# A decoder layer on one core: adaLN modulation from transposed weights, and eight accumulators in the first projection pass

## The chip, the cores and the metric

The kernel runs on one core of one Trainium2 chip. The metric is the device time of one execution in microseconds (us): 1293.14 us before, the median of three runs (1292.88 to 1295.22). One further execution was profiled. All views below are of that one.

The engines of the core run side by side and wait for one another by semaphores: TensorE (PE; PEld is its weight load), VectorE (DVE), ScalarE (ACT), GpSimd (POOL), and SyncE (SP), whose queue issues the DMA transfers.

## The reference, cut to what matters

```python
c_act = silu(c)                              # c: (1, 1024)
mod = c_act @ w_ada + b_ada                  # w_ada: (1024, 6144)
sh1, sc1, g1, sh2, sc2, g2 = split(mod, 6)   # 1024 numbers each
h = x * (1 + sc1) + sh1                      # x: (1024 tokens, 1024)
proj = h @ w_in                              # columns q, kc, vc, ksl, vsl, kwn, vwn, gt, u, v
# kc, vc -> compressed keys and values; v -> gelu, norm, spatial gating with u
# attention (compressed, selected, window), gating, output projection, layer norm
h = x * (1 + sc2) + sh2
out = layer_norm(ALPHA * x + (1 + g2) * ((silu(h @ w1) * (h @ w3)) @ w2))
```

Everything is float32. The kernel multiplies with a high and a low part of each operand: one product tile takes three matmuls, high by high, high by low, low by high (`mm3`, lines 91 to 98).

## The kernel before, in words

The beginning of the kernel makes `h` and multiplies it with the columns `v`, `kc` and `vc` of `w_in`. The model dimension (1024) is cut into eight blocks `k` of 128. For each block, the kernel needs 128 values of `sc1` and of `sh1`, one per partition (`mod`), and the block of `x` with the model dimension on the partitions.

**Modulation.** `load_ada` (153) loads, for each block `k`, the 1024 rows of `w_ada` by 128 columns of `sh1` and of `sc1`, in pieces of 512 bytes. The sum over the 1024 rows is made in two steps. POOL sums the first three groups of 128 rows (325 to 329), DVE the last five (222, 223), DVE adds the two (336). TensorE then transposes the 128 x 256 sum (232) and DVE adds along the row (235) and adds the bias (239). One block at a time is done so (the pair 4 and 5 together, `GR`).

**x.** `load_x` loads `x` with tokens on the partitions. TensorE transposes it, four 128 x 128 pieces to a PSUM tile (`make_t`, 256). ACT makes the high part of `h` from it (243), ACT or DVE the float32 value (245, 247), DVE or POOL the low part (`affine_split`, 241).

**The two passes.** PSUM holds eight banks. In the first pass (lines 322 to 345) there are accumulators for four token tiles of `v` and for `kc` and `vc` over the first 512 tokens, six banks; the others serve the transposes. A block of the first pass is 18 matmuls with 512 columns. The second pass (391 to 401) does the same for the other 512 tokens. ACT and DVE empty the accumulators behind each pass: the copies `kT` (403) and the gelu `vn` (358).

**Behind the passes** come the key compression (`cmp_blk`, `cmp_mm`; line 496 builds its input from `kT` on DVE and POOL), the products with `u` (`pu`), the transposes of `w_s` (`pws`, from `ws`, which POOL masks in line 557), then V, the gates, K and Q (`pq`, with DVE's part in line 686). In between, `bgstep` puts one background step at a time: `ada_row` for `g1`, and `ada_tiles` with `ada_cols` for `sh2` and `sc2`. These last two are 16 row sums on DVE (lines 222 and 223, 128 x 1024 each), then 16 transposes on TensorE (232) into the PSUM tag that `pq` uses too, and DVE's row sums (235).

**What sets the order.** Program order is the priority; a scheduler orders each engine's instructions, and `order` pins one behind another (the loads of the beginning are pinned in a chain, `dseq`). SBUF tiles come from pools: `B` has 41 buffers, `RAW` four; the PSUM tag `g` has three banks, `ot` one, `s` four.

Of the kernel before, what the change touches and what calls it, by code (L numbers as in the profile page):

```python
# [16 lines left out]
S = 1024  # L17
# [14 lines left out]
GR = ((0, 1), (1, 1), (2, 1), (3, 1), (4, 2), (6, 1), (7, 1))  # L32
# [3 lines left out]
UA, PK = 6, 3  # L36
# [7 lines left out]
def hymba_kernel(ctx, tc, x, c, w_ada, b_ada, w_in, cmp_pos, cmp_w1, cmp_w2, vn_g, vn_b, w_s, b_s,  # L44
                 out_g, w_o, ln1_g, ln1_b, w1, w3, w2, ln2_g, ln2_b, out):
# [93 lines left out]
    rows = B("rows")  # L139
    dseq(rows[0:8, 0:128], c.rearrange("o (k p) -> (o k) p", p=128))  # L140
    dseq(rows[0:48, 128:256], b_ada.rearrange("o (k p) -> (o k) p", p=128))
    pc = G("pc")
    nc.tensor.transpose(out=pc[:, 0:8], in_=rows[0:8, 0:128], identity=ident[0:8, 0:8])
    ccol = cst.tile([128, 8], F32, name="ccol")
    V_.tensor_copy(ccol, pc[:, 0:8])
# [3 lines left out]
    V_.tensor_scalar(cact, cact, 0.5, None, MULT)  # L149

    adat, xt = {}, []

    def load_ada(q, n):
        for k4 in range(0, NK, 4 // n):
            t = B("ada")
            tv = t.rearrange("p (k a n) -> p k a n", k=4 // n, a=2)
            for a in range(2):
                dseq(tv[:, :, a, :], w_ada[k4 * 128:(k4 + 4 // n) * 128, a * 1024 + q * 128:a * 1024 + (q + n) * 128]
                     .rearrange("(k p) n -> p k n", p=128))
            for k in range(4 // n):  # L160
                adat[q, k4 + k] = t[:, k * 256 * n:(k + 1) * 256 * n]

    def load_x(hf, j):
        xb = B("x")
        dseq(xb.rearrange("p (t n) -> p t n", t=4),
             x[hf * 512:(hf + 1) * 512, j * 256:(j + 1) * 256].rearrange("(t p) n -> p t n", p=128))
        xt.append(xb)
# [7 lines left out]
    wvr, wkr, wv, wkc, lastw = [], [], [], [], []  # L175

    def load_wv(k2):
        wvr.append(B("wvr"))
        dseq(wvr[k2].rearrange("p (k n) -> p k n", k=2),
             w_in[k2 * 256:(k2 + 1) * 256, OFF["v"]:OFF["v"] + 512].rearrange("(k p) n -> p k n", p=128))  # L180

    def load_wkc(k2):
        wkr.append(RAW("wkr")[:, 0:512])
# [3 lines left out]
    def split_start(q):  # L187
        if q % 2 == 0:
            h, l = split(wvr[q // 2])
            for i in range(2):  # L190
                wv.append((h[:, i * 512:(i + 1) * 512], l[:, i * 512:(i + 1) * 512]))
            h, l = split(wkr[q // 2], 512)
            lastw.append(lasts[0])
            for i in range(2):
                wkc.append((h[:, i * 256:(i + 1) * 256], l[:, i * 256:(i + 1) * 256]))
# [16 lines left out]
    cols = cst.tile([128, 80], F32, name="cols")
    pc = G("pc")
    nc.tensor.transpose(out=pc[:, 0:48], in_=rows[0:48, 128:256], identity=ident[0:48, 0:48])
    V_.tensor_copy(cols[:, 0:48], pc[:, 0:48])
    posT = cst.tile([128, 64], F32, name="posT")
    bcol, l1g, l1b, og, bs = cols[:, 0:48], cols[:, 48:56], cols[:, 56:64], cols[:, 64:72], cols[:, 72:80]
    mod = cst.tile([128, 4, 8], F32, name="mod")
# [6 lines left out]
    def ada_cols(acc, m, j0, c0, n):  # L225

        r = sml.tile([128, 2, n], F32, name="adr")
        p = [G("pm") for _ in range(n // 2)] or [G("pm")]
        for a in range(2):
            for i in range(n):  # L230
                z = a * n + i
                nc.tensor.transpose(out=p[z // 4][:, z % 4 * 128:(z % 4 + 1) * 128], in_=acc[:, a, i * 128:(i + 1) * 128], identity=ident)
        for z, pp in enumerate(p):
            w = min(2 * n, 4)
            V_.tensor_reduce(out=r.rearrange("p a i -> p (a i)")[:, z * 4:z * 4 + w],
                             in_=pp[:, 0:w * 128].rearrange("p (i q) -> p i q", q=128), op=ADD, axis=AX)
        for a in range(2):
            j = j0 + a
            V_.scalar_tensor_tensor(mod[:, m + a, c0:c0 + n], r[:, a, :], float(a), bcol[:, j * 8 + c0:j * 8 + c0 + n], ADD, ADD)
# [12 lines left out]

# [15 lines left out]
    def start_mm(k, hf):  # L268
        for t in range(4):
            sl = slice(hf * 512 + t * 128, hf * 512 + (t + 1) * 128)  # L270
            mm3(acc4[t // 2][:, t % 2, :], (hH[k][:, sl], hL[k][:, sl]), wv[k], k == 0, k == NK - 1)
# [1128 lines left out]
```

## Time and profile before

| | |
|---|---|
| median of three runs | 1293.14 us |
| the profiled execution | 1295.98 us |
| its span, first to last instruction | 1293.9 us |
| PE busy | 1217.3 us, 94% of the span |
| DVE busy | 978.1 us, 76% |
| mean granted TensorE clock | 0.986 |
| DMA | 188.09 MB, mean 145 GB/s |

The span is what the views are drawn on; the execution's time is 2.1 us longer. A matmul's shown duration overlaps the next one's, so that a matmul's share of TensorE's time is read from start to start.

### The profile page before, as it was taken

To read this page: it belongs to the slowest core of one execution; us is meant where nothing else is said; L and a number is where in the kernel's file an instruction comes from. 1 tells how busy PE (TensorE), PEld (TensorE's weight loads), DVE (VectorE), ACT (ScalarE), POOL (GpSimd) and SP (SyncE) were. 2 spreads that over 40 slices of the span, in tenths; PEclk is the share of its full clock that TensorE was granted. 3 is DMA by queue.
4 is the path that set the end of the run, shared out by engine and by line. 5 is a ranking of instruction groups with operands and counts; after the bars stand their busy time and mean duration, and the time that the engine had idled before them with its cause. 6 is when DMAs were issued, how large, how long until landed. Compare 5 with 4: busy or idle time off the path is not lost. (4 is left out here: it accounts for less than half of the span.)

```text
span 1293.9 us, 17271 instructions
## 1 busy us (share of the span) xinstructions
PE 1217.3 (94%) x5980; PEld 1007.1 (78%) x5980; DVE 978.1 (76%) x1702; ACT 569.3 (44%) x1040; POOL 396.2 (31%) x400
## 2 busy tenths in 40 slices
PE   5899999899999999999789999999999989999994
PEld 3687797778888888878567788888788868888873
DVE  5746887959999999868767867667767668785487
ACT  2343422349888998113623323333323225454131
POOL 5332213325655674301132233232233230000123
PEclk8999999999999999999999999999999999999997
DMA  9821453901000002554335645556554579687252
GB/s 288 266 66 50 140 157 101 242 3 66 1 2 1 1 2 73 201 177 128 114 123 170 188 169 165 179 188 187 169 194 142 178 229 342 238 274 258 58 202 81
DMA packets 148011, 188.09 MB, mean 145 GB/s; under 512 B 17402, under 2 KB 95314, under 8 KB 147924
## 3 DMA queue, kind: packets, MB, share of 16 engines
q1 hardware_dynamic: 147924, 187.00, 45.4%
q8 instruction: 47, 0.77, 0.2%
q14 instruction: 40, 0.33, 0.1%
HBM read 136.11 MB, written 48.76 MB: 143 GB/s over the span
## 5 line engine op out<-in xcount | busy, mean ns | idle before, releaser
L777 POOL TENSOR_SCALAR P<-P,ast,gate 128x640 f32<-128x640 f32 (+7 forms) x128 | 99.6, 785 | 66.5 <-DVE ast L776 50.0
L107 DVE TENSOR_TENSOR wL<-cr,wH 128x1024 fp32r<-128x1024 f32 x77 | 99.7, 1318 | 24.8 <-ACT wH L102 24.5
L1058 POOL TENSOR_TENSOR w2r<-w2r,g2r 128x512 f32<-128x512 f32 x44 | 60.9, 1399 | 169.2 <-DMA w2r<-in_w 84.6
L102 ACT ACTIVATE wH<-cr 128x1024 fp32r<-128x1024 f32 x77 | 79.9, 1059 | 70.9 <-DMA cr<-combP 63.1
L107 DVE TENSOR_TENSOR pt<-pt,pt 128x512 fp32r<-128x512 f32 (+1 forms) x148 | 99.9, 682 | 7.0 <-ACT pt L102 6.3
L710 ACT ACTIVATE P<-P,ast 128x640 f32<-128x640 f32 (+7 forms) x128 | 93.8, 734 | 1.7 <-DVE ast L709 1.2
L102 ACT ACTIVATE pt<-pt 128x512 fp32r<-128x512 f32 (+1 forms) x148 | 87.1, 592 | 16.3 <-PE pt L128 13.7
L1169 POOL TENSOR_TENSOR pt<-pt,pt 128x512 f32<-128x512 f32 x22 | 35.0, 1592 | 164.4 <-ACT pt L1168 164.4
L128 PE MATMUL pt<-ident,P 128*128 128x128 f32 x528 | 78.9, 272 | 0.2 <-DVE pt L107 0.2
L1124 DVE TENSOR_TENSOR h<-h,pt 128x512 f32<-128x512 f32 x33 | 26.4, 799 | 66.1 <-POOL pt L1171 65.7
L128 PEld LDWEIGHTS pt<-ident,P 128*128 128x128 f32 x528 | 65.1, 140 | 12.7 <-issue 0.5
L1112 PE MATMUL pcd<-wH,wH 128*128 128x512 f32 x176 | 69.2, 395 | 4.7 <-ACT pt L1163 2.4
L102 ACT ACTIVATE wH<-raw 128x1024 fp32r<-128x1024 f32 (+2 forms) x41 | 42.3, 1040 | 69.8 <-DMA combP<-wt 20.4
L1276 PE MATMUL py<-wH 128*128 128x512 f32 x176 | 68.6, 394 | 2.6 <-DVE r L1215 2.6
L1112 PE MATMUL pa<-h2H,wH 128*128 128x512 f32 x176 | 68.9, 392 | 0.8 <-ACT pt L1147 0.3
L1114 PE MATMUL pa<-h2H,wL 128*128 128x512 f32 x176 | 68.9, 391 | 0.7 <-DVE wL L107 0.7
L1113 PE MATMUL pcd<-wL,wH 128*128 128x512 f32 x176 | 69.2, 393 | 0.0
L1114 PE MATMUL pcd<-wH,wL 128*128 128x512 f32 x176 | 69.0, 392 | 0.0
L1276 PE MATMUL py<-wH,wL 128*128 128x512 f32 x176 | 69.0, 393 | 0.0
L1276 PE MATMUL py<-wL,wH 128*128 128x512 f32 x176 | 68.9, 392 | 0.0
L1113 PE MATMUL pa<-h2L,wH 128*128 128x512 f32 x176 | 68.5, 389 | 0.0
L107 DVE TENSOR_TENSOR wL<-raw,wH 128x1024 fp32r<-128x1024 f32 (+2 forms) x41 | 51.6, 1265 | 19.8 <-ACT wH L102 15.9
(323 smaller groups left out, 3671.3 us busy)
## 6 DMA issues: line engine op xcount, KB each, us to landing
cr<-combP SPq DMA_DIRECT2D x77, 512.0 KB, 4.9
ada<-in_w_ada SPq DMA_DIRECT2D x96, 256.0 KB, 4.2
raw<-in_w SPq DMA_DIRECT2D x48, 512.0 KB, 4.9
w2r<-in_w SPq DMA_DIRECT2D x44, 256.0 KB, 2.8
combP<-wt SPq DMA_DIRECT2D x44, 256.0 KB, 3.5
combP<-as SPq DMA_DIRECT2D x44, 256.0 KB, 2.4
combP<-w2r SPq DMA_DIRECT2D x33, 256.0 KB, 2.0
combP<-h SPq DMA_DIRECT2D x33, 256.0 KB, 3.9
```

The costliest lines, as they stand in the source:

```text
L102: A_.activation(o, i, AF.Copy)
L107: return V_.tensor_tensor(o, i, f(h), SUB)
L128: nc.tensor.transpose(out=p[:, j * 128:(j + 1) * 128], in_=src(j), identity=ident)
L710: A_.activation(P, P, AF.Exp, scale=-1.0, bias=nm, accum_out=den)
L777: P_.tensor_scalar(P, P, st[:, 2, hh:hh + 1], gcol(i, h, br), MULT, MULT)
L1058: P_.tensor_tensor(r[z][a], r[z][a], rowt["g2r"][:, a * 512:a * 512 + 512], MULT)
L1112: nc.tensor.matmul(o, lh, rh, start=start and i == 0, stop=False, skip_group_check=not start)
L1113: nc.tensor.matmul(o, lh, rl, start=False, stop=False, skip_group_check=not start)
L1114: r = nc.tensor.matmul(o, ll, rh, start=False, stop=i == 3, skip_group_check=not start)
L1124: V_.tensor_tensor(s, s, c, MULT)
L1169: P_.tensor_tensor(p5, p5, p7, ADD)
L1276: lastm[0] = nc.tensor.matmul(o, x_[:, ts_], y_[:, 512:1024], start=not cont and p == 0 and n == 0, stop=p == NP - 1 and n == 2, skip_grou ...
```

## The change: what it does

The host lays out three more inputs: `xT`, the transpose of `x`; `w_adaT`, the transpose of `w_ada`; and `colsT`, 128 x 152, with `c`, the biases, the norm gains, `b_s` and `cmp_pos` as columns.

- `c` is loaded to all 128 partitions (`crow`), and its silu is made there, 128 x 1024 (a factor 0.5 left out, which `scale` puts back). For one block of `sc1` or `sh1`, 128 rows of `w_adaT` are loaded, 512 KB in rows of 4 KB, and one DVE instruction multiplies them with `crow` and sums along the row, with the bias as start: `mod_col`, two for each block. In the trace of before, an instruction of this kind is in line 709 (there with add and minimum). It is followed by a short one that reads the sum out.
- The transposes of `x` and of the row sums, POOL's part of the sums, and the transposes of the small columns are gone.
- The first pass takes the first 768 tokens for `v` (six accumulators) and the first 512 for `kc` and `vc`: eight banks, 24 matmuls a block. The second pass takes the last 256 tokens for `v` and the last 512 for `kc` and `vc`: 12 matmuls a block.
- ACT makes both the high part and the float32 value of `h` from the loaded `xT` (in place), DVE all low parts. `chain` pins the order on ACT and on DVE in the first pass.
- The background sums for `sh2` and `sc2` become 16 `mod_col` steps; `ada_cols` and the empty steps behind the sums are gone.

```diff
-GR = ((0, 1), (1, 1), (2, 1), (3, 1), (4, 2), (6, 1), (7, 1))
+W1 = 768
-    rows = B("rows")
-    dseq(rows[0:8, 0:128], c.rearrange("o (k p) -> (o k) p", p=128))
...
+    crow = B("crow")
+    dseq(crow, c[0:1].to_broadcast([128, 1024]))
+    cols = cst.tile([128, 152], F32, name="cols")
+    dseq(cols, colsT)
+    A_.activation(th, crow, AF.Tanh, scale=0.5)
+    V_.scalar_tensor_tensor(crow, th, 1.0, crow, ADD, MULT)
...
+    def mod_col(m, j, k, t):
+        return V_.tensor_tensor_reduce(out=t, in0=t, in1=crow, scale=0.5, scalar=bcol[:, j * 8 + k:j * 8 + k + 1], op0=MULT, op1=ADD,
+                                accum_out=mod[:, m, k:k + 1])
...
+    load_wv(0)
+    for k in range(NK):
+        if k % 2:
+            if k < 7:
+                load_wv(k // 2 + 1)
+                load_wkc(k // 2 + 1)
+        load_ada(k)
+        load_x(k, 0, W1)
+        if k == 0:
+            load_wkc(0)
+    for k in range(NK):
+        load_x(k, W1, S)
...
-    acc4 = [S2("pv0") for i in range(2)]
+    accv = [s_[:, a, :] for s_ in (S2("pv0"), S2("pv0")) for a in range(2)] + [G("pv1"), G("pv1")]
     acck = [OT("pkc"), G("pvc")]
-    for q, n in GR:
-        split_start(q)
...
+    for k in range(NK):
+        for j in (1, 0):
+            chain("V", mod_col(j, j, k, adat[j, k]))
+        if k == 0:
+            split_start(0)
+        if k % 2 and k < 7:
+            split_start(k // 2 + 1)
+        make_h(k, 0, 512, W1)
+        start_mm(k, range(6), accv, 0, acck)
...
         if hf:
+            for k in range(NK):
+                make_h(k, W1, S)
...
-            pt = make_t(0, 1)
             for k in range(NK):
-                make_h(k, 1, pt)
...
+                start_mm(k, (6, 7), accv, 1, acck)
...
-        bgs[0].append(lambda hf=hf, acc_=acc_: ada_cols(acc_().rearrange("p (a n) -> p a n", a=2), 2, 3, hf * 4, 4))
+    def ada_col(m, j, k):
+        t = RAW("ada")
+        load(t, w_adaT[j * 1024 + k * 128:j * 1024 + (k + 1) * 128], 3)
+        mod_col(m, j, k, t)
```

The instructions move at three places that matter below. A row of the order is a line, an operation, out<-in by the program's names with buffer numbers, and a shape.

DVE at block 0 of the first pass, before:

```order
L222 TENSOR_SCALAR pt_213<-ada_92,cact 128x256
L223 SCALAR_TENSOR_TENSOR pt_213<-ada_95,cact,pt_213 128x256 x4
L336 TENSOR_TENSOR pt_213<-pt_213,pt_214 128x256
L235 TENSOR_REDUCE adr<-pm_234 128x2
L239 SCALAR_TENSOR_TENSOR mod<-adr,cols 128x1 x2
L107 TENSOR_TENSOR wL_206<-wvr_100,wH_205 128x1024
L107 TENSOR_TENSOR wL_210<-wkr_102,wH_209 128x512
L107 TENSOR_TENSOR hL_193<-h_240,hH_185 128x512
```

and now (`ISA` with `ada`, `crow` is the multiply-and-sum, `ISA mod` its read-out):

```order
L158 ISA ada_105,mod<-ada_105,crow_81,cols 128x1024
L158 ISA mod 128x1
L158 ISA ada_107,mod<-ada_107,crow_81,cols 128x1024
L158 ISA mod 128x1
L107 TENSOR_TENSOR wL_192<-wvr_103,wH_191 128x1024
L107 TENSOR_TENSOR wK_193<-pt_110,wK_193 128x512
L107 TENSOR_TENSOR hL_175<-x_95,hH_167 128x512
L107 TENSOR_TENSOR hL_175<-x_95,hH_167 128x256
```

Five row sums over 256 columns, an addition, a reduction and the bias have become two instructions over 1024 columns with their read-outs; they stand ahead of the same splits of the weights, and the low part of `h` is now 768 wide.

TensorE at the start, before:

```order
L128 MATMUL pt_228<-ident,x_98 128x128 x4
L232 MATMUL pm_234<-ident,pt_213 128x128 x2
L128 MATMUL pt_259<-ident,x_98 128x128 x4
L92 MATMUL pv_201<-wH_205,hH_185 128x512
L95 MATMUL pv_201<-wL_206,hH_185 128x512
L92 MATMUL pv_202<-wH_205,hH_185 128x512
L95 MATMUL pv_202<-wL_206,hH_185 128x512
L92 MATMUL pkc_203<-hH_185,wH_209 128x512
L92 MATMUL pvc_204<-hH_185,wH_209 128x512
L96 MATMUL pv_201<-wH_205,hL_193 128x512
```

and now:

```order
L92 MATMUL pv_183<-wH_191,hH_167 128x512
L92 MATMUL pv_184<-wH_191,hH_167 128x512
L92 MATMUL pkc_187<-hH_167,wK_193 128x512
L95 MATMUL pv_183<-wL_192,hH_167 128x512
L95 MATMUL pv_184<-wL_192,hH_167 128x512
L92 MATMUL pv_185<-wH_191,hH_167 128x512
L95 MATMUL pv_185<-wL_192,hH_167 128x512
L92 MATMUL pv_186<-wH_191,hH_167 128x512
L95 MATMUL pv_186<-wL_192,hH_167 128x512
L92 MATMUL pvc_188<-hH_167,wK_193 128x512
L96 MATMUL pv_183<-wH_191,hL_175 128x512
```

The transposes (`pt`, `pm`) ahead of and between the products are gone, and the fifth and sixth accumulator (`pv_185`, `pv_186`; `pv_183` and `pv_184` hold two each) take part in the block.

DVE in the Q products, at the end of the background sums, before:

```order
L222 TENSOR_SCALAR acc_2125<-ada_2122,cact 128x1024
L223 SCALAR_TENSOR_TENSOR acc_2125<-ada_2127,cact,acc_2125 128x1024
L235 TENSOR_REDUCE adr<-pm_2079 128x4
L686 SCALAR_TENSOR_TENSOR Q_1957<-pq_2049,Q_1957 64x512
L107 TENSOR_TENSOR pt_2135<-raw_2131,pt_2134 128x512
L235 TENSOR_REDUCE adr<-pm_2080 128x4
L239 SCALAR_TENSOR_TENSOR mod<-adr,cols 128x4
L223 SCALAR_TENSOR_TENSOR acc_2125<-ada_2171,cact,acc_2125 128x1024
L686 SCALAR_TENSOR_TENSOR Q_1961<-pq_2049,Q_1961 64x512
```

and now:

```order
L639 SCALAR_TENSOR_TENSOR Q_1712<-pq_1731,Q_1712 64x512
L158 ISA ada_1837,mod<-ada_1837,crow_81,cols 128x1024
L158 ISA mod 128x1
L639 SCALAR_TENSOR_TENSOR Q_1716<-pq_1731,Q_1716 64x512
L158 ISA ada_1840,mod<-ada_1840,crow_81,cols 128x1024
L158 ISA mod 128x1
L158 ISA ada_1872,mod<-ada_1872,crow_81,cols 128x1024
L158 ISA mod 128x1
L639 SCALAR_TENSOR_TENSOR Q_1714<-pq_1766,Q_1714 64x512
```

The reductions `adr` of the transposed sums no longer stand between DVE's parts of Q; where a row sum stood, a multiply-and-sum and its read-out stand.

## Rows read from the trace of the kernel before

**Rows 1.** The page: busy us, share of the span, instructions.

```profile
PE 1217.3 (94%) x5980; PEld 1007.1 (78%) x5980; DVE 978.1 (76%) x1702; ACT 569.3 (44%) x1040; POOL 396.2 (31%) x400
```

**Rows 2.** Stretches: busy us (instructions) by engine, TensorE clock, DMA share, GB/s.

```profile
10.00:20.00 10.00, 8.39 (x28) 6.22 (x28) 6.33 (x14) 2.91 (x4) 5.23 (x9) 1.00 1.15 310
20.00:30.00 10.00, 5.37 (x16) 3.82 (x16) 7.06 (x15) 2.91 (x4) 5.72 (x8) 0.71 1.12 330
...
50.00:60.00 10.00, 10.00 (x50) 8.20 (x49) 7.84 (x17) 4.34 (x7) 0.00 (x0) 1.00 0.85 275
```

**Rows 3.** TensorE in order of time: start us, us, instruction, [idle before <-releaser].

```profile
14.27 0.80 PE L92 MATMUL pv<-wH,hH 128*128 128x512 f32 x1 [0.86 <-ACT hH L243]
...
17.41 0.39 PE L92 MATMUL pv<-wH,hH 128*128 128x512 f32 x1
17.64 0.40 PE L95 MATMUL pv<-wL,hH 128*128 128x512 f32 x1
...
26.50 0.80 PE L92 MATMUL pv<-wH,hH 128*128 128x512 f32 x1
...
31.44 0.39 PE L92 MATMUL pv<-wH,hH 128*128 128x512 f32 x1
...
106.91 0.39 PE L96 MATMUL pvc<-hH,wL 128*128 128x512 f32 x1
```

**Rows 4.** TensorE groups, first 63.6 us, then 63.6 to 107.2 us: count, busy, mean ns.

```profile
L92 PE MATMUL pv<-wH,hH 128*128 128x512 f32 x28 | 12.9, 461 | 3.8 <-ACT hH L243 3.7
L128 PE MATMUL pt<-ident,x 128*128 128x128 f32 x32 | 6.3, 333 | 8.3 <-DMA x<-in_x 7.2 <-DVE adr L235 1.0
...
L92 PE MATMUL pv<-wH,hH 128*128 128x512 f32 x36 | 14.5, 402 | 0.9 <-ACT vn L358 0.9
```

**Rows 5.** All engines in order of time: first work on loaded data.

```profile
10.62 1.12 PE L128 MATMUL pt<-ident,x 128*128 128x128 f32 x4 [7.24 <-DMA x<-in_x]
...
11.98 1.06 ACT L102 ACTIVATE wH<-wvr 128x1024 fp32r<-128x1024 f32 x1 [8.81 <-DMA wvr<-in_w_in]
...
13.46 0.76 ACT L243 ACTIVATE hH<-pt,mod 128x512 fp32r<-128x512 f32 x1
```

**Rows 6.** VectorE groups of the whole run: line, tiles, shape, count, busy us, mean ns.

```profile
L709 DVE CUSTOM_DVE_ANT_0 P<-ps,distm 128x1024 f32<-128x1024 f32 x8 | 9.7, 1209 | 0.0
L709 DVE DVE_READ_ACCUMULATOR2_ANT ast<- 128x1 f32 x192 | 16.0, 83 | 0.0
L107 DVE TENSOR_TENSOR wL<-wvr,wH 128x1024 fp32r<-128x1024 f32 x4 | 4.9, 1224 | 0.5 <-ACT wH L102 0.5
L365 DVE TENSOR_REDUCE st<-vn 128x16 f32<-128x1024 f32 x4 | 4.8, 1211 | 0.0
L107 DVE TENSOR_TENSOR hL<-h,hH 128x512 fp32r<-128x512 f32 x8 | 5.5, 689 | 5.4 <-ACT h L245 5.4
L107 DVE TENSOR_TENSOR V<-pvg,V 128x256 fp32r<-128x256 f32 x8 | 3.3, 422 | 1.9 <-ACT V L102 1.9
```

**Rows 7.** Line 223 alone: ns min/median/max.

```profile
L223 DVE SCALAR_TENSOR_TENSOR acc<-ada,cact,acc x28: 1239/1280/2644, 168.7 to 551.1; 128x1024 f32<-128x1024 f32 x28
```

**Rows 8.** TensorE, 245 to 253 us.

```profile
245.12 0.60 PE L766 MATMUL ps<-KL,Q 128*128 128x256 f32 x2
248.97 0.50 PE L92 MATMUL pq<-hH,pt 128*128 128x512 f32 x1 [3.25 <-DVE adr L235]
...
250.01 0.63 PE L92 MATMUL pq<-hH,pt 128*128 128x512 f32 x1
250.43 0.63 PE L95 MATMUL pq<-hL,pt 128*128 128x512 f32 x1
...
252.95 0.40 PE L95 MATMUL pq<-hL,pt 128*128 128x512 f32 x1
```

**Rows 9.** The stretch from 200 to 262 us.

```profile
200.00:262.00 62.00, 57.93 (x260) 46.83 (x259) 51.29 (x70) 18.14 (x28) 21.03 (x9) 0.97 0.65 170
```

**Rows 10.** TensorE behind the second pass.

```profile
113.21 1.09 PE L128 MATMUL pws<-ident,ws 128*128 128x128 f32 x8 [2.06 <-POOL ws L557]
```

More of the change, by code (lines that the diff above doesn't have):

```diff
@@ L44, in hymba_kernel @@
 def hymba_kernel(ctx, tc, x, c, w_ada, b_ada, w_in, cmp_pos, cmp_w1, cmp_w2, vn_g, vn_b, w_s, b_s,
-                 out_g, w_o, ln1_g, ln1_b, w1, w3, w2, ln2_g, ln2_b, out):
+                 out_g, w_o, ln1_g, ln1_b, w1, w3, w2, ln2_g, ln2_b, xT, w_adaT, colsT, out):
     nc = tc.nc
@@ L137, in dseq @@
         seq[0] = d
-    rows = B("rows")
-    dseq(rows[0:8, 0:128], c.rearrange("o (k p) -> (o k) p", p=128))
[L141 to L145, printed above, removed]
+    crow = B("crow")
+    dseq(crow, c[0:1].to_broadcast([128, 1024]))
+    cols = cst.tile([128, 152], F32, name="cols")
+    dseq(cols, colsT)
+    ccol, bcol, l1g, l1b, og, bs, posT = [cols[:, a:b] for a, b in
+                                          ((0, 8), (8, 56), (56, 64), (64, 72), (72, 80), (80, 88), (88, 152))]
+    th = B("th")
+    A_.activation(th, crow, AF.Tanh, scale=0.5)
+    V_.scalar_tensor_tensor(crow, th, 1.0, crow, ADD, MULT)
+    for j in (1, 4):
+        V_.tensor_scalar(bcol[:, j * 8:j * 8 + 8], bcol[:, j * 8:j * 8 + 8], 1.0, None, ADD)
     cact = cst.tile([128, 8], F32, name="cact")
@@ L149, in hymba_kernel, with chain, load_ada, load_x @@
     V_.tensor_scalar(cact, cact, 0.5, None, MULT)
[L151 to L167, printed above, removed]
+    mod = cst.tile([128, 4, 8], F32, name="mod")
+    def mod_col(m, j, k, t):
+        return V_.tensor_tensor_reduce(out=t, in0=t, in1=crow, scale=0.5, scalar=bcol[:, j * 8 + k:j * 8 + k + 1], op0=MULT, op1=ADD,
+                                accum_out=mod[:, m, k:k + 1])
+    adat, xt = {}, [B("x") for _ in range(NK)]
+    last = {}
+    def chain(e, i):
+        if e in last:
+            order(i, last[e])
+        last[e] = i
+    def load_ada(k):
+        for j in (1, 0):
+            t = adat[j, k] = B("ada")
+            dseq(t, w_adaT[j * 1024 + k * 128:j * 1024 + (k + 1) * 128])
+    def load_x(k, a, b):
+        dseq(xt[k][:, a:b], xT[k * 128:(k + 1) * 128, a:b])
     def split(raw, n=1024):
@@ L182, in load_wkc @@
     def load_wkc(k2):
-        wkr.append(RAW("wkr")[:, 0:512])
+        wkr.append(H2(F32, "pt"))
         dseq(wkr[k2].rearrange("p (k n) -> p k n", k=2),
              w_in[k2 * 256:(k2 + 1) * 256, OFF["kc"]:OFF["kc"] + 256].rearrange("(k p) n -> p k n", p=128))
[L187 to L195, printed above, removed]
@@ L212, in hymba_kernel, with split_start @@
[L212 to L218, printed above, removed]
+    def split_start(k2):
+        h, l, t = B("wH", F32R), B("wL", F32R), B("wK", F32R)
+        chain("A", A_.activation(h, wvr[k2], AF.Copy))
+        chain("A", A_.activation(t[:, 0:512], wkr[k2], AF.Copy))
+        chain("V", sub(l, wvr[k2], h))
+        chain("V", sub(t[:, 512:1024], wkr[k2], t[:, 0:512]))
+        for i in range(2):
+            wv.append((h[:, i * 512:(i + 1) * 512], l[:, i * 512:(i + 1) * 512]))
+            wkc.append((t[:, i * 256:(i + 1) * 256], t[:, 512 + i * 256:512 + (i + 1) * 256]))
@@ L223, in ada_fma @@
         return V_.scalar_tensor_tensor(acc, w, cact[:, k:k + 1], acc, MULT, ADD)
[L225 to L239, printed above, removed]
@@ L265, in OT, with start_mm @@
     def OT(nm="ot"):
         return psg.tile([128, 512], F32, tag="ot", name=nm_(nm), bufs=1)
[L268 to L271, printed above, removed]
+    def start_mm(k, ts, vs, hf, ks):
+        for t, o in zip(ts, vs):
+            sl = slice(t * 128, (t + 1) * 128)
+            mm3(o, (hH[k][:, sl], hL[k][:, sl]), wv[k], k == 0, k == NK - 1)
```

103 lines of the change are left out of this document (28 added, 75 removed).

## The prediction

> **What bounds the kernel now.** I read the page first: TensorE is busy for 94% of the span [rows 1]. A gain must take work off TensorE or fill its gaps, and the gaps are at the beginning. The table of stretches shows them: from 10 to 30 us TensorE is busy for 8.4 and 5.4 of 10 us while the DMA engines are full (share above 1.1, 310 to 330 GB/s); from 50 us on it is full [rows 2]. The list in order of time gives the two ends: the first product starts at 14.27 us, the last of the second pass at 106.91 us, so that pass ends at 107.1 [rows 3].
>
> I take these 93 us apart. A matmul of 512 columns goes from start to start in 0.23 us at full clock (17.41 to 17.64) [rows 3] and in 0.42 at half (250.01 to 250.43) [rows 8]. The groups give 28 + 36 high-by-high products of `v`, a third of 192; `kc` and `vc` add half as many, 288 in all [rows 4]. At 0.228 that is 65.7 us. Eight products `pu`, pulled ahead of the pass's end, are 1.8. The 64 transposes of `x` (32 of them in the first group [rows 4]) and 16 of the sums, at about 0.1 each, are 8 (74 of them behind 14.27: 7.4). Two spells at half clock, 14.27 to 17.41 and 26.50 to 31.44 [rows 3], lose half of their 8 us, 4. Together 78.9; the other 14 us TensorE waited. The second spell follows a gap in its work, and the clock of that slice is 0.71 [rows 2].
>
> **The start.** Ahead of the first product now stand `crow`, `cols`, a block of `wv`, two tiles of `w_adaT`, 768 tokens of `x` and a block of `kc, vc` weights: 2.83 MB. Before, `x` was there at 10.62 us (1.6 MB issued) and `wv` at 11.98 (2.13 MB) [rows 5]. At 0.33 MB/us the missing 0.7 MB add 2.1 us, which makes 14.1; two small loads, each with its own landing, no longer go first, for which I take 0.8 off (an estimate). So the last piece lands at about 13.3. ACT works in a pinned order: it splits that piece (0.6 us) ahead of `hH` (0.76 [rows 5]). What queues behind ACT's wait is `hH`, and TensorE waits for it. First product at 15 us, against 14.27 (bounds 13.5 and 17).
>
> **The first pass.** Each engine's work for one block, from rows: TensorE 24 x 0.228 = 5.5 us. The loads 12.45 MB over the seven other blocks, 1.78 MB each, at 0.33 MB/us 5.4 us. DVE: two multiply-and-sums, for which the kind in line 709 shows 1.21 us and 0.08 for the read-out, 2.6; `hL` 0.69 + 0.42; half of a weight split, 0.95; together 4.65 [rows 6]. ACT: twice 0.76 [rows 5] and about 0.45 for the narrower piece, plus 0.8 of split, 3.2. So TensorE and the loads run level and the rest is cover. TensorE: 15 + 192 x 0.228 + 1.6 for a first spell at half clock as long as before (3.1 us) = 60.4. The loads: 13.3 + 12.45 / 0.33 = 51.0, then 2.1 for the last sums and `hH`, then the block's 5.5: 58.6. Level, TensorE a little later: the pass ends at 60.5 with the handover of the first blocks. If the loads only made 308 GB/s, 61.5.
>
> What is added here: DVE's sum waits for each tile of `w_adaT`, and behind it wait the splits of weights and `hL`, for which TensorE waits; this is in the sum, as DVE has 0.9 us to spare in a block. The short row of `x` for the second pass (eight loads of 128 KB) comes last in SP's queue, lands 3 us behind, and is needed at 60.
>
> **The second pass.** It starts in the bank that `kc` leaves, so it waits for DVE's copy `kT`; `vc` and the first `v` bank wait for ACT (copy, table load, gelu), with 20 products of `kc` and `vc`, 4.6 us, ahead of them. I take 0.5 us. Then 96 x 0.228 = 21.9. End at 82.9 us, 24.2 us ahead of 107.1 (bounds 20 and 27). All low parts of this half are now DVE's instead of GpSimd's, eight times 0.42 [rows 6]; TensorE's 22 us cover them. The eight `pu` products come behind instead of ahead, 1.8 us, but TensorE waited 2.06 us there for GpSimd's mask of `ws` [rows 10], so nothing is lost. The chain from `kT` to the compression starts at the copy, and moves with it.
>
> **The background sums.** Sixteen of them stand between V and Q. Removed on TensorE: 16 transposes, 1.6 us; the wait of 3.25 us of `pq` for DVE's reduction `adr` (same PSUM tag) at 245 to 249; and the spell at half clock behind it, 248.97 to 252.95, where nine or ten products take 0.42 instead of 0.23, 1.8 us [rows 8]. That is 6.6. What could be late next is DVE: it is busy for 51.3 of 62 us there [rows 9]. A Q product takes TensorE 24 x 0.228 = 5.5 us, and DVE then has two sums (2.6), two parts of Q (1.4) and part of a split (0.6), 4.6. It fits, but with little room; I take 5.8 of the 6.6 (bounds 1.5 and 7).
>
> **Sum.** 24.2 + 5.8 = 30 us. Span 1293.9 - 30 = 1263.9. The profiled execution took 1295.98, 2.8 above the median of 1293.14, and I take the 30 off the median: 1263 us. Behind 300 us the order of the instructions is all but unchanged; I give that 1.5 us either way.
>
> **The price I cannot read.** Line 709's instruction takes one operand from PSUM. Here both are float32 in SBUF. Lower bound: 1.21 us for the row, as there. Upper: product and sum as two passes, 1.22 + 1.21 [rows 6], or the slowest two-operand row, 2.64 [rows 7]. The nearest row is line 223, which also reads two float32 rows from SBUF with a scalar, median 1.28 [rows 7]; with that the first pass is unchanged, DVE's block being 4.8 us. I take 1.21 to 1.28.
>
> The Trainium skill speaks against it: "Vector Engine (DVE) Microarchitecture Reference", in "Points that are easy to get wrong", says that the two-source form with accumulator runs at half throughput when both sources come from SBUF and are not bf16. By that rule the sum would take about 2.4 us, and the result would be the second rival's. Line 223 is not halved, but it has no accumulator output, so that no row here decides.
>
> **Rivals.**
> 1. The loads set the pace of the first pass. For it: they are full now, and run level with TensorE in my sum. Against: their rows grow from 512 bytes to 3 and 4 KB. At 260 GB/s, under every full stretch of [rows 2], the last block has its data at 13.3 + 47.9 + 2.1 and the pass ends at 68.8: 8.3 us of the gain go, 1271.
> 2. Two passes on DVE, 2.5 us with the read-out. A block is then 7.05 us of DVE; the first tile of `w_adaT` is there at about 10 us, the sums of the last block end at 10 + 7 x 7.05 + 5 = 64.4, the first pass with `hH` and the block's products at 70.7, the second at 93.1: the gain is 14. In the background, 16 x 1.2 = 19 us more of DVE meet 10.7 idle us [rows 9]: about 8.5 lost instead of 5.8 gained. 1293 - 5.5 = 1287.5.
> 3. Slower: the same mechanism at a higher price P. The second pass then ends at about 53 + 16 P (93.1 at 2.5), the background loses 16 (P - 1.3) - 10.7, so that the change loses from P = 2.7 us on; TensorE would also wait over 2 us in each block and could lose its clock as at 26.5. At P = 3 us: 10 us lost, 1303. Against it: no row of 128 x 1024 comes to 2.7; 2.64 is a maximum beside GpSimd, which is idle here.
> 4. It does not do what it says: the gain of the start is given back, since the compression waits for its weights as before. For it: these are DVE- and load-heavy stages. Against: those loads wait for buffers that are freed by the same earlier work. 1291 to 1294.
> 5. More: the loads at 350 GB/s, a start at 13.5, no wait at the banks, and an easier DVE behind: 1254 to 1257.
>
> **How the numbers follow.** The forecast, 1258 to 1268: 62%. Rival 1: 12%, rival 2: 12%, rival 3: 4%, rival 4: 3%, rival 5: 7%. The predicted time is 1263. The range takes in most of rivals 1 and 5: 1255 to 1276; rivals 2 to 4 lie above it. About 0.2% (2.6 us) is what a measurement of this kernel tells from no change. Faster by more than that: 0.94; within it: 0.02; slower: 0.04.
>
> **What would show it.** Right: the first product near 15 us, its second block without a wait, the last product of the second pass near 83 us, the multiply-and-sum at 1.2 to 1.3 us, no wait of `pq` above 1 us, no half clock there. Wrong: a multiply-and-sum near 2.4 us and TensorE waiting for `hH` in each block (rival 2); waits of DVE for `w_adaT` in each block (rival 1); a new wait of `pq` for DVE's parts of Q.

## The result: 34 us less, in the two places where less was expected

The changed kernel takes 1259.60 us (median of four runs, 1257.97 to 1261.56), the kernel before, beside it, 1294.18. The ratio is 0.9724, 95% interval 0.9707 to 0.9740. Forecast were 1263 us and 30 us less, in a range of 1255 to 1276. The profiled execution took 1261.56 us, with a span of 1259.8 (before: 1295.98 and 1293.9). On another chip, later, the change gave 1257.74 against 1297.01, ratio 0.970 (0.968 to 0.972).

The same views after the change follow. First the page's line of busy time, which answers to [rows 1].

```profile
PE 1196.9 (95%) x5880; PEld 994.4 (79%) x5880; DVE 964.6 (77%) x1686; ACT 581.2 (46%) x1065; POOL 355.8 (28%) x357
```

A hundred TensorE instructions are gone, and 20.4 us of its busy time (products at half clock count in it); the other 14 us of the gain were gaps. The stretches, as in [rows 2], show which:

```profile
10.00:20.00 10.00, 5.78 (x18) 4.66 (x19) 8.78 (x14) 5.61 (x9) 0.00 (x0) 1.00 1.04 398
20.00:30.00 10.00, 10.00 (x46) 8.26 (x45) 7.57 (x14) 5.44 (x10) 0.00 (x0) 1.00 1.04 398
30.00:40.00 10.00, 10.00 (x46) 8.29 (x45) 7.57 (x13) 6.41 (x10) 0.00 (x0) 1.00 1.04 401
```

TensorE is full from 20 us on, and the loads run at 398 to 401 GB/s, not at the 310 to 330 of before. The list of TensorE in order of time, for [rows 3] and [rows 10]:

```profile
14.22 1.22 PE L92 MATMUL pv<-wH,hH 128*128 128x512 f32 x2 [14.22 <-ACT hH L232]
15.24 0.63 PE L92 MATMUL pkc<-hH,wK 128*128 128x512 f32 x1
15.67 1.05 PE L95 MATMUL pv<-wL,hH 128*128 128x512 f32 x2
...
17.38 0.50 PE L92 MATMUL pv<-wH,hH 128*128 128x512 f32 x1
17.72 0.40 PE L95 MATMUL pv<-wL,hH 128*128 128x512 f32 x1
17.95 0.40 PE L92 MATMUL pvc<-hH,wK 128*128 128x512 f32 x1
...
81.23 0.39 PE L96 MATMUL pvc<-hH,wK 128*128 128x512 f32 x1
81.45 0.39 PE L92 MATMUL pu<-wH,hH 128*128 128x512 f32 x1
...
87.56 0.66 PE L128 MATMUL pws<-ident,ws 128*128 128x128 f32 x4 [0.51 <-POOL ws L510]
```

The first product starts where it did (14.22; before 14.27) and the last of the second pass 25.7 us earlier (81.23; before 106.91). Between them no product waits long enough to carry a bracket; the mask of `ws` costs 0.51 us where it cost 2.06. Up to 17.38 us the products are 0.43 us apart (15.24 to 15.67), as at half clock elsewhere. That this is the low level is read from the spacing alone, in [rows 3] too: the granted clock of the stretch from 10 to 20 us reads 1.00 before and after. Next the multiply-and-sum, all 32 of them (ns min/median/max), the price that [rows 6, 7] could only bound (the whole kernel, background included):

```profile
L158 DVE CUSTOM_DVE_ANT_0 ada<-ada,crow,cols x32: 1275/1280/2653, 9.8 to 226.5; 128x1024 f32<-128x1024 f32 x32
L158 DVE DVE_READ_ACCUMULATOR2_ANT mod<- x32: 76/83/88, 11.0 to 227.7; 128x1 f32 x32
```

The rest of the gain lies between K and attention. This is the stretch from the last product of K to the first of attention's compressed part (`ot<-pt,vcm`), first before, then after (columns as in [rows 2]):

```profile
227.30:290.90 63.60, 57.62 (x260) 46.31 (x260) 47.84 (x78) 24.18 (x46) 19.27 (x17) 0.97 0.46 121
```

```profile
202.30:256.60 54.30, 53.72 (x246) 43.31 (x244) 38.61 (x74) 23.08 (x44) 18.59 (x17) 1.00 0.42 109
```

It is 9.3 us shorter. TensorE stood idle for 6.0 us of it before and for 0.6 now, and the granted clock is 1.00 where it was 0.97. TensorE's waits (total, times, longest), first one before, besides that of `pq` in [rows 8], and then after the change, from 80 to 300 us, where no `pq` is left:

```profile
PE ps L764 <- DVE ast L709: 2.1, 3, 1.0
```

```profile
PE hid L95 <- DVE wL L107: 1.5, 2, 0.9
...
PE ps L717 <- DVE ast L662: 0.4, 2, 0.2
```

So the shift is 25.7 us at the end of the second pass, 25.0 at the end of K, 34.3 at attention's first compressed product (290.9, now 256.6) and 34.1 at the end. From there to the end it is 1003.0 us before and 1003.2 after; the changed kernel run again took 1000.5, so that the agreement to 0.2 us is chance.

### The profile page after: what moved, and what is told of

The parts are those of the page before. It is cut to its first block, busy times and chain, and to the rows that moved or that the text cites. A ratio compares the mean times of both kernels' runs of the same rounds, so it can differ in the third digit from the quotient of the medians.

```text
span 1259.8 us, 16940 instructions
## 1 busy us (share of the span) xinstructions
PE 1196.9 (95%) x5880; PEld 994.4 (79%) x5880; DVE 964.6 (77%) x1686; ACT 581.2 (46%) x1065; POOL 355.8 (28%) x357
## 5 line engine op out<-in xcount | busy, mean ns | idle before, releaser
L1011 POOL TENSOR_TENSOR w2r<-w2r,g2r 128x512 f32<-128x512 f32 x44 | 61.5, 1414 | 168.3 <-DMA w2r<-in_w 80.2
L107 DVE TENSOR_TENSOR wL<-raw,wH 128x1024 fp32r<-128x1024 f32 (+2 forms) x41 | 49.0, 1199 | 18.0 <-ACT wH L102 16.2
```

Source lines behind the costliest of these rows:

```text
L107: return V_.tensor_tensor(o, i, f(h), SUB)
L1011: P_.tensor_tensor(r[z][a], r[z][a], rowt["g2r"][:, a * 512:a * 512 + 512], MULT)
```

## The experiments

All compare with the kernel before on the same chip. A mark is the start of an instruction in the profiled execution: the first product, the last product of the second pass, and attention's first compressed product.

| kernel | us, median | ratio to before (95%) | first product | last of 2nd pass | attention |
|---|---|---|---|---|---|
| before | 1294.18 | | 14.27 | 106.9 | 290.9 |
| changed | 1259.60 | 0.9724 (0.9707 to 0.9740) | 14.22 | 81.2 | 256.6 |
| changed, again | 1257.74 | 0.970 (0.968 to 0.972) | 13.49 | 80.6 | 256.2 |
| e1 old background | 1272.14 | 0.9818 (0.9801 to 0.9835) | 12.8 | 81.8 | 267.4 |
| e2 four accumulators | 1262.15 | 0.974 (0.9722 to 0.9758) | 13.3 | 85.1 | 260.6 |
| e3 x alone | 1306.02 | 1.0074 (1.0058 to 1.009) | 15.6 | 115.0 | 300.9 |
| e9 x alone, held | 1291.09 | 0.9959 (0.9944 to 0.9974) | 15.8 | 99.4 | 285.7 |
| e4 short rows | 1265.42 | 0.9758 (0.9738 to 0.9778) | 13.7 | 83.8 | 259.8 |
| e6 warm | 1260.25 | 0.972 (0.9702 to 0.9739) | 13.13 | 80.4 | 257.5 |
| e7 start order | 1259.91 | 0.9717 (0.9697 to 0.9737) | 12.48 | 79.7 | 255.2 |
| e8 both | 1262.19 | 0.9735 (0.9715 to 0.9756) | 17.7 | 83.0 | 259.6 |
| e10 two passes | 1282.52 | 0.990 (0.9878 to 0.9922) | 15.67 | 103.3 | 279.1 |
| e11 longer chain | 1263.83 | 0.9752 (0.9729 to 0.9775) | 12.83 | 83.0 | 259.1 |
| e12 lead | 1262.52 | 0.9734 (0.9709 to 0.9758) | 13.0 | 79.1 | 258.7 |

The first product of the same instructions starts anywhere from 12.8 to 14.2 us, so a difference of under a microsecond there says nothing.

**e1, the background sums as before.**

```diff
...
-            bgs[0].append(lambda a=a, k=k: ada_col(2 + a, 3 + a, k))
...
+        ada_tiles(lambda k, a, hf=hf: w_ada[...], acc_)
+        bgs[0].append(lambda hf=hf, acc_=acc_: ada_cols(acc_()..., 2, 3, hf * 4, 4))
```

> The changed kernel, but the shift and scale of the second norm are again summed over eight tiles per half on VectorE, turned over by 16 TensorE transposes and reduced, as before the change. Theory A (this part of the change gave what the first pass did not: 34.1 us in all less 25.7 us at the end of the second pass, so 8 to 9 us): 1267 to 1269 us, with a wait of 2 to 3.5 us of a pq product for the reduction adr and half clock behind it. The term as predicted, 5.8 us: about 1265.5 us. Theory B (the wait and the slow clock in that stage came from the old start, not from this part): 1259 to 1261.5 us, no wait over 1 us.

Theory A holds for the mechanism; the time, 1272.14, is 3 us above its range. The second pass ends 0.6 us after the changed kernel's, and attention starts 10.8 us later. TensorE in order of time shows the wait and the slow products of [rows 8] again, at another time of the program:

```profile
225.47 0.50 PE L92 MATMUL pq<-hH,pt 128*128 128x512 f32 x1 [3.25 <-DVE adr L237]
...
228.02 0.63 PE L95 MATMUL pq<-hL,pt 128*128 128x512 f32 x1
228.45 0.63 PE L96 MATMUL pq<-hH,pt 128*128 128x512 f32 x1
...
229.68 0.39 PE L96 MATMUL pq<-hH,pt 128*128 128x512 f32 x1
229.91 0.39 PE L92 MATMUL pq<-hH,pt 128*128 128x512 f32 x1
```

The wait is the same 3.25 us, the products behind it are 0.43 us apart and then 0.23. The waits of `ps` for `ast` are back at 2.1 us too. From the last product of K to attention it is 63.6 us again (203.8 to 267.4), the length of before, where the changed kernel takes 54.3. So this part is worth 9.3 us by itself, not 5.8. Of the rest of the 10.8 us a stretch at half clock ahead of that stage takes the most (granted clock 0.95 from 118.2 to 149.6 us, 1.00 in the changed kernel's same work); its cause is open.

**e2, four accumulators in the first pass.**

```diff
-W1 = 768
+W1 = 512
...
-        start_mm(k, range(6), accv, 0, acck)
+        start_mm(k, range(4), accv, 0, acck)
```

> The changed kernel with 512 positions in the first pass (four V accumulators and one of the two K banks' halves filled as before) and 512 in the second, so 18 products a block in the first pass, not 24; the number of products stays 288. Theory A (TensorE is what bounds, and the loads at 400 GB/s bring 1.65 MB in 4.1 us, as fast as 18 products take): a little slower, 1260.5 to 1263.5 us, from VectorE's 4.3 us a block against 4.1 us of products and from the banks that the second pass wants back at once. Theory B (loads at the 330 GB/s of the sum: 5.0 us a block against 4.1): 1265 to 1269 us. Theory C (eight accumulators do nothing): within 1 us of 1259.6 us.

The time is theory A's, but its reason was not. The last product of the second pass starts 4.5 us later than in the changed kernel run again, though the loads are as fast (396 to 400 GB/s). VectorE in order of time, then TensorE:

```profile
29.90 1.28 DVE L158 CUSTOM_DVE_ANT_0 ada<-ada,crow,cols 128x1024 f32<-128x1024 f32 x1
...
34.13 0.69 DVE L107 TENSOR_TENSOR hL<-x,hH 128x512 fp32r<-128x512 f32 x1 [1.73 <-ACT x L234]
34.74 1.28 DVE L158 CUSTOM_DVE_ANT_0 ada<-ada,crow,cols 128x1024 f32<-128x1024 f32 x1
...
39.57 1.28 DVE L158 CUSTOM_DVE_ANT_0 ada<-ada,crow,cols 128x1024 f32<-128x1024 f32 x1
```

```profile
33.30 0.50 PE L92 MATMUL pv<-wH,hH 128*128 128x512 f32 x1 [0.20 <-ACT hH L232]
...
38.14 0.50 PE L92 MATMUL pv<-wH,hH 128*128 128x512 f32 x1 [0.20 <-ACT hH L232]
```

A block comes every 4.83 us on VectorE (29.90, 34.74, 39.57) and every 4.84 on TensorE, whose 18 products need 4.1. VectorE is not busy all that time: it waits 1.73 us for ScalarE in every second block. What sets the pace is a chain. VectorE's multiply-and-sums give a block's scale and shift, ScalarE rounds `x` with them, VectorE subtracts, and only then, in VectorE's order, come the sums of the next block. In the changed kernel the same chain looks like this, first VectorE, then ScalarE:

```profile
26.45 1.03 DVE L107 TENSOR_TENSOR hL<-x,hH 128x512 fp32r<-128x512 f32 x2 [2.08 <-ACT x L234]
27.40 1.28 DVE L158 CUSTOM_DVE_ANT_0 ada<-ada,crow,cols 128x1024 f32<-128x1024 f32 x1
...
28.60 1.28 DVE L158 CUSTOM_DVE_ANT_0 ada<-ada,crow,cols 128x1024 f32<-128x1024 f32 x1
...
31.98 1.03 DVE L107 TENSOR_TENSOR hL<-x,hH 128x512 fp32r<-128x512 f32 x2 [0.35 <-ACT x L234]
32.92 1.28 DVE L158 CUSTOM_DVE_ANT_0 ada<-ada,crow,cols 128x1024 f32<-128x1024 f32 x1
```

```profile
29.93 1.31 ACT L232 ACTIVATE hH<-x,mod 128x512 fp32r<-128x512 f32 x2 [1.54 <-DVE mod L158]
31.14 1.29 ACT L234 ACTIVATE x<-x,mod 128x512 f32<-128x512 f32 x2
```

From 27.40 to 32.92 it is 5.52 us a block, and 24 products take 24 x 0.228 = 5.47. With eight accumulators TensorE has just enough to do to cover the chain, and they are worth these 4.5 us.

**e11, a longer chain.** One more multiply of 512 columns per block, whose output nothing uses.

```diff
         make_h(k, 0, 512, W1)
+        chain("V", V_.tensor_tensor(adat[0, k][:, 0:512], adat[1, k][:, 0:512], crow[:, 0:512], MULT))
```

> The changed kernel with one more VectorE multiply of 512 columns (0.69 us, its output not used) behind the subtraction of each block of the first pass, ahead of the next block's multiply-and-sum. Theory A (VectorE, ScalarE and VectorE again follow one another and take 5.52 us a block, as long as the products): 6.1 to 6.3 us a block, and 2.5 to 5 us more than 1257.7. Theory B (VectorE has 0.85 us of room in a block, 4.65 us of work against 5.5 of products): no more than 0.5 us.

Theory A: VectorE's blocks start at 15.56, 21.68 and 27.80 us, 6.12 apart, and from the fifth block on TensorE waits for each (the first of these waits below).

```profile
15.56 1.27 DVE L158 CUSTOM_DVE_ANT_0 ada<-ada,crow,cols 128x1024 f32<-128x1024 f32 x1
...
21.68 1.28 DVE L158 CUSTOM_DVE_ANT_0 ada<-ada,crow,cols 128x1024 f32<-128x1024 f32 x1
```

```profile
37.32 0.50 PE L92 MATMUL pv<-wH,hH 128*128 128x512 f32 x1 [0.20 <-ACT hH L232]
```

Against the changed kernel run again the second pass ends 2.4 us later and attention starts 2.9 us later, at the lower end of the forecast; the median is 6.1 us higher, above it (another chip; by the ratios to before, 0.5 points, 6.7 us). The profiled execution, the fastest of its four, is 1261.40 against 1258.44, and these 3.0 us are all ahead of attention (behind it 1000.6 and 1000.5). What the slower executions lost, no trace shows.

**e10, multiply and sum as two instructions.**

```diff
-            chain("V", mod_col(j, j, k, adat[j, k]))
+            chain("V", mod_col2(j, j, k, adat[j, k]))
...
+        i = V_.tensor_tensor(t, t, crow, MULT)
+        chain("V", i)
+        i = V_.tensor_reduce(out=r, in_=t, op=ADD, axis=AX)
+        chain("V", i)
+        return V_.tensor_scalar(mod[:, m, k:k + 1], r, 0.5, bcol[:, j * 8 + k:j * 8 + k + 1], MULT, ADD)
```

> The changed kernel with the multiply-and-sum of the first pass as two instructions (multiply, then sum along the row, then scale and bias on one column): 2.6 to 2.7 us more of VectorE a block. Theory A (a block's multiply-and-sum, the roundings on ScalarE that need it and VectorE's subtraction behind them follow one another, 5.52 us a block in the traces of the changed kernel, with 2.1 us of waiting of VectorE in it): the first multiply of a block follows that of the block before by 8.1 to 8.4 us, and the time is 15 to 20 us more than 1257.7. Theory B (only VectorE's busy time counts, 4.65 us a block and 2.65 more): 7.2 to 7.5 us a block and 10 to 14 us more. Theory C (products and loads hide it): within 2 us.

The period is theory A's, 8.38 us (VectorE, the first of the two instructions), and TensorE waits 1.0 to 2.65 us in most blocks:

```profile
17.80 1.22 DVE L163 TENSOR_TENSOR ada<-ada,crow 128x1024 f32<-128x1024 f32 x1
...
20.44 1.22 DVE L163 TENSOR_TENSOR ada<-ada,crow 128x1024 f32<-128x1024 f32 x1
...
26.19 1.22 DVE L163 TENSOR_TENSOR ada<-ada,crow 128x1024 f32<-128x1024 f32 x1
...
34.57 1.22 DVE L163 TENSOR_TENSOR ada<-ada,crow 128x1024 f32<-128x1024 f32 x1
```

```profile
32.45 0.50 PE L92 MATMUL pv<-wH,hH 128*128 128x512 f32 x1 [2.63 <-ACT hH L240]
```

The loss is 24.8 us (another chip), above the 15 to 20 forecast: the second pass ends 22.7 us later, 2.2 of them because the first product does. A sum takes 2.64 us from start to start (17.80 to 20.44), where it took 1.20 (27.40 to 28.60): 16 x 1.44 = 23 us. Nothing of that was hidden. The granted clock falls behind such waits, too (0.66 from 40 to 45 us), as rival 3 reckoned with.

**e3 and e9, x alone.** The kernel before, with only `x` transposed by the host; e9 also holds the second half's roundings behind the first's.

```diff
...
-        p = G("pt")
-        trans4(p, lambda j: xt[hf * 4 + k // 2][...])
-        return p
+        return xt[k][:, hf * 512:hf * 512 + 512]
```

> The kernel before, with x alone laid out transposed by the host: 64 of its transposes in the two passes are gone, the modulation is still summed over tiles on VectorE and GpSimd and turned over by transposes. Theory A (the modulation sums set the pace of the first pass, and TensorE waited there; only the transposes of the second pass, 32 x 0.1 us, were on its path): 1289 to 1292 us. Theory B (the transposes and the evictions that read them were on the path in both passes): 64 x 0.1 us and their bank waits, 1284 to 1288 us. Theory C (x was most of it: the half-clock spell goes too): under 1280 us.

All three theories missed: it is slower by 0.7% (0.6 to 0.9). ScalarE's list of waits names why (total, times, longest):

```profile
ACT hH L243 <- DMA x<-in_xT: 18.1, 1, 18.1
```

Without transposes nothing ties the second half's rounding to the second pass. In ScalarE's order it moved ahead of work of the first, and everything behind it waited for a load at the end of the queue.

> The run of the transposed x alone once more, with the roundings of the second half of x held behind those of the first half on ScalarE and VectorE: in the run before, ScalarE stood 18 us at a rounding that waited for the second half of x. Theory A (the modulation sums set the pace of the first pass, so the transposes of x there cost little): 1289 to 1292 us. Theory B (the transposes were on the path in both passes): 1283 to 1288 us. Theory C (without a planned order this part alone still gains nothing): 1293 us or more.

With the order held it is 5.2 us faster than before, theory A's range, a seventh of the change's gain. The marks speak less clearly for A: the second pass ends 7.5 us earlier, twice A's 3.2. Between there and attention 2.4 us are given back, in two stages with a lower granted clock (0.94 from 135.9 to 166.8 us, before 1.00 in the same work; 0.95 from 221.0 to 285.8, before 0.97). Up to 60 us TensorE waits for the sums (`pm` for `pt`, 12.7 us in all; before, 4.1, and 7.2 for the load of `x`). What the new form of the first pass's modulation gives by itself no run shows, as no kernel has it without the transposed `x`.

**e4, short rows.**

```diff
...
-            dseq(t, w_adaT[j * 1024 + k * 128:j * 1024 + (k + 1) * 128])
+            dseq(t.rearrange("p (q n) -> p q n", n=128), w_adaS[j * 8 + k].rearrange("q p n -> p q n"))
```

> The changed kernel with the transposed x and modulation weights of the first pass laid out so that each partition's row comes in pieces of 512 B, not in one of 3 or 4 KB; same bytes, same number of transfers. Theory A (the length of the rows gave the 400 GB/s): 310 to 340 GB/s from 20 to 40 us; 5.3 to 5.7 us of loads a block against 5.5 of products, so the products wait little, 1260 to 1263 us, with the first product 0.5 to 1.5 us later. Theory B (the rate has another cause): 390 to 400 GB/s and 1259 to 1260.5 us.

Theory A on the rate: with pieces of 512 B the loads fall to 308 GB/s, just under its range, in the stretch that had 398:

```profile
20.00:30.00 10.00, 10.00 (x46) 8.27 (x45) 6.85 (x12) 5.95 (x10) 0.00 (x0) 1.00 1.18 308
```

Now VectorE waits for a tile and TensorE behind it (one line of each):

```profile
41.33 1.28 DVE L158 CUSTOM_DVE_ANT_0 ada<-ada,crow,cols 128x1024 f32<-128x1024 f32 x1 [1.23 <-DMA ada<-in_w_adaS]
```

```profile
45.42 0.50 PE L92 MATMUL pv<-wH,hH 128*128 128x512 f32 x1 [1.75 <-ACT hH L232]
```

The second pass ends 2.6 to 3.2 us later, attention starts 3.2 to 3.6 later. The first product, at 13.7, is not 0.5 to 1.5 us later, as was forecast. The median is 1265.42, above the 1260 to 1263 forecast.

**e5 to e8 and e12, an earlier start.** e5 is the changed kernel again:

> The changed kernel again, beside the three that follow, so that they are compared on one chip: 1258 to 1262 us on every theory, first product at 14.2 us, end of the second pass at 81.4 to 81.6 us. The number of half-clock spells between 590 and 670 us (three in the profile after, one or two in others) may differ; each costs 3.4 us at half pace, 1.7 us.

The time, 1257.74, is 0.3 us under this range; the first product and the end of the second pass come 0.7 and 0.6 us earlier than forecast.

e6 lets TensorE work ahead of the first product:

```diff
+            for _ in range(12):
+                nc.tensor.matmul(acck[1], wv[0][0][:, 0:128], wv[0][0], start=True, stop=True)
```

> The changed kernel with twelve more 128x512 products of the first weight block into a bank that is overwritten later, put before the first product that counts; they need only the first rounded weights, which are there at 9.6 us. Theory A (the granted clock is low at the first products because TensorE did nothing before them): the spacing of the products from 14.2 us on is 0.23 us at once, not 0.43, the second pass ends 1.6 us earlier at 79.9 us, and the time is 1.2 to 1.8 us less. Theory B (the second block's loads set its start, or the extra products delay the first): 0 to 0.5 us less, with a wait of 1 us or more before the second block.

```profile
8.14 5.15 PE L300 MATMUL pvc<-wH 128*128 128x512 f32 x12 [8.14 <-ACT wH L199]
13.13 0.63 PE L92 MATMUL pv<-wH,hH 128*128 128x512 f32 x2
13.60 0.39 PE L92 MATMUL pkc<-hH,wK 128*128 128x512 f32 x1
13.83 0.40 PE L92 MATMUL pvc<-hH,wK 128*128 128x512 f32 x1
...
58.75 0.47 PE L92 MATMUL pkc<-hH,wK 128*128 128x512 f32 x1 [1.60 <-ACT x L234]
```

Theory A is right on the pace: the twelve extra products are 0.42 us apart, and the counted ones behind them 0.23 at once (by the spacing; the granted clock reads 1.00 here as well). But the second pass then waits 1.60 us, put down to ScalarE, which is at the end of the same chain; VectorE's copy `kT`, which frees the bank, ends at the same time (58.6 us), behind its own subtractions that wait for ScalarE. The pass ends only 0.2 us earlier. Theory B named a wait of this size, but ahead of the second block. No theory has the time: 1260.25 (1259.61 to 1260.67) is 2.5 us more than on the same chip without the edit, 1.3 of it ahead of attention.

e7 loads the first modulation tiles ahead of the first weights and rounds `x` ahead of the K weights:

> The changed kernel with the first two modulation tiles and the first x loaded ahead of the first weights of V, and the rounding of x ahead of the split of the K weights on ScalarE. Theory A (what comes ahead of the first product in the queue and on ScalarE sets its start): first product at 11.5 to 12.7 us, second pass ends at 79 to 80.3 us, 1 to 2.5 us less time. Theory B (the bytes ahead of the first product are the same, so it starts when the last of them is there): first product at 13.7 to 14.3 us, no difference in time.

First product 12.48, second pass and attention both 0.9 us earlier than in e5: theory A in the marks, at the lower end. In the time nothing of it is left: 1259.91 (1258.13 to 1261.13) against 1257.74 (1256.67 to 1259.25) on the same chip.

> The edits of the two kernels before this one together. Theory A (the gains don't add, since the second block cannot start before its modulation tiles are there at about 17 to 18.5 us): second pass ends at 78.5 to 80 us, 1.5 to 3 us less than the changed kernel. Theory B (they add): 77 to 78 us and 3 to 4.5 us less. Theory C (neither does anything): within 0.5 us.

None of the three. The extra products need the first rounded weights, which the other edit makes late (12.42 us); they then stand 5.5 us in the way.

e12 shortens the chain: e7's order, transposes of the activated row ahead of the first product, and one sum of the sixth and of the eighth block in the gap where VectorE waited 2.08 us.

```diff
...
+    for _ in range(28):
+        nc.tensor.transpose(out=acck[1][:, 0:128], in_=crow[:, 0:128], identity=ident)
...
+            if (k, j) not in ((5, 1), (7, 1)):
+                chain("V", mod_col(j, j, k, adat[j, k]))
+        if k in (4, 6):
+            chain("V", mod_col(1, 1, k + 1, adat[1, k + 1]))
```

> The changed kernel with the loads and ScalarE's order of the run start_order, 28 transposes of the activated row of c ahead of the first product (into a bank that is overwritten later; they need a row that is there at 7.6 us), and the scale's multiply-and-sum of the sixth and eighth block moved ahead of the subtraction of the block before, where VectorE waited 2.1 us. Theory A (the start and the slow clock are worth 2.6 us once the chain of VectorE and ScalarE is shorter): first product at 12.4 to 12.8 us at 0.23 us spacing, end of the second pass at 78.3 to 79.5 us against 81.0, attention 1.5 to 2.5 us earlier. Theory B (the loads of the second block or the chain hold the first pass as before): end of the second pass at 80 to 81 us. The whole time: 1 to 3 us less than 1257.7 by theory A, where the half-clock spells behind 590 us, 1.7 us each, can take it back.

Theory A up to the second pass, which ends 1.5 us earlier than in e5 (the first product, at 13.04, is later than forecast). Attention nevertheless starts 2.5 us later. Of the 4.0 us lost between, 1.2 are in the compression. VectorE waits there for a load, first in e5, then in e12 (total, times, longest):

```profile
DVE cb L479 <- DMA cb<-in_cmp_w: 2.2, 1, 2.2
```

```profile
DVE cb L491 <- DMA cb<-in_cmp_w: 3.5, 1, 3.5
```

The low part `wL` stands behind that copy in VectorE's list, and a product waits for it:

```profile
115.53 0.39 PE L95 MATMUL hid<-wL,wH 128*128 128x256 f32 x1 [1.19 <-DVE wL L107]
```

The load is issued 1.5 us earlier than in e5 (109.2 for 110.7), but VectorE can go on only 0.2 us earlier (113.98 for 114.18). In e6 and e8 the same wait is 3.8 and 3.4 us long, and the product waits 1.46 us (all that e6 loses up to attention) and 1.08. Why the load takes longer in these three is open. Another 1.6 us are in the next stage, at half clock:

```profile
130.00:140.00 10.00, 9.45 (x43) 7.87 (x44) 3.12 (x9) 2.50 (x8) 0.00 (x0) 0.83 0.43 145
```

The last 1.2 are between K and attention (55.5 us for 54.3), half of them two waits of `pq` for VectorE (0.43 and 0.15). No version tried beats the changed kernel.

## Why the prediction held, step by step

- **The price.** Taken 1.21 to 1.28 us, measured 1.28 in the median, and in all 16 sums of the first pass, beside which GpSimd is idle. Three in the background took 2.10 to 2.65 us, each beside a GpSimd instruction, though others beside one took 1.28. By the Trainium skill's rule ("Vector Engine (DVE) Microarchitecture Reference", "Points that are easy to get wrong") it would be about 2.4, by the prediction's estimate. The trace does not agree, for two float32 sources in SBUF are not halved here; it doesn't tell whether this instruction is the form that the rule means. Rivals 2 and 3 fall with the measured price.
- **The start.** Taken 15 us, measured 14.22 and 13.49. The last piece was there at 12.84 instead of 13.3, as the loads were faster than 0.33 MB/us; the forecast's own terms, 13.3 + 0.6 + 0.76, make 14.7. No run shows the 0.8 us taken off for the two small loads.
- **The first pass.** Its size was right: the second pass starts at 81.45 - 96 x 0.228 = 59.6 us, forecast 60.5. The step "DVE has 0.9 us to spare in a block" failed. It added up VectorE's busy time, 4.65 us, and left out that VectorE waits for ScalarE in the middle of it. The chain is 5.52 us long (e2, e10, e11), as long as the products, so there was no room, and the pass held only because the price stayed at the lower bound. That was luck: the prediction counted on room that wasn't there. Rival 2's end of the second pass, reckoned in the same way (53 + 16 P), would be 95.2 us at 2.64 us a sum; in e10, at that price, the last product starts at 103.3, so it was 8 us too early. The 1.6 us for the slow first products fit as a size, but without them the pass ends only 0.2 us earlier (e6), since the chain stands right behind.
- **The loads.** "At 0.33 MB/us" failed as well, to the good side: 0.40, from the longer rows (e4). At 308 GB/s (e4) the second pass starts at 62.2 us; the forecast said 61.5 for that rate.
- **Second pass.** Taken 0.5 us of bank wait, measured none; last product at 81.23, so the end at 81.5, forecast 82.9.
- **The eight `pu` products** cost nothing, as said.
- **The background sums.** Taken 5.8 us, measured 9.3. The removed pieces came out as read: `pq` 3.25, half clock 1.8, transposes 1.6. Left out were the `ps` waits for `ast` (2.1 us before, 0.4 now) and 0.5 us of `pm`, outside the stretch of [rows 8]. Together that is 8.9 of the 9.3. The 0.8 taken off for a fuller VectorE was not lost: it is busy for 38.6 of 54.3 us there, where it was for 47.8 of 63.6.
- **Sum.** 24.2 + 5.8 were forecast, 25.7 + 9.3 measured, less 0.7 lost between. That the rest would stand still held to 0.2 us in the profiled execution, and to 2.5 in the same kernel run again. The forecast came out 3 us high because both terms were too small: the first by 0.8 us at the start and 0.5 at the banks, the second by the waits left out and the 0.8 taken off.

## What to carry to other kernels

Before calling an engine's busy time "cover", follow one block through all engines: if A waits for B in the middle of its own list, the chain's length is what has to fit, and it can be as long as the pace while the engine shows 24% idle, as VectorE did from 20 to 40 us. When work is taken off, look for the waits of everything that shares the engine it ran on, not only for the wait it caused itself. And when a transposition is what tied a piece of work to its place in time, removing it needs an order in its stead (e3).

## What was not expected of the hardware

- Loads by one queue ran at 398 to 401 GB/s where most rows are 3 and 4 KB long, and at 308 with pieces of 512 B, same bytes, same number of transfers.
- The time behind attention, in the one profiled execution of each kernel, differs by up to 6 us, though all edits lie ahead of it: 1000.0 us in e8, 1006.0 in e12. The profile's record of the granted clock doesn't explain it. It holds half-clock spells between 500 and 1240 us that add up to 17.1 us in both of these, in the changed kernel (1003.2) and in e6 (1001.0), and to 10.2 in e2 (1000.2) and in the changed kernel run again (1000.5). The five executions of e12 alone reach from 1259.27 to 1266.41 us, and the profiled one is the slowest, so that this need not be a difference between kernels. A gain of 1 us at the start, as e7's, cannot be read from the whole time here.
